# A new start for a fused decoder trunk: c spread by one DMA, x scaled on ScalarE, first scale and shift columns on ScalarE, products of zeros ahead

## The chip, the cores and the metric

The kernel runs on one core of one Trainium2 chip. The metric is device time in microseconds (us) of one execution. One execution is also taken by the hardware profiler; its span and the trace behind it are what the text reads. The engines have short names: PE is the matrix engine (PEld its weight loads), DVE the vector engine, ACT the scalar (activation) engine, POOL the general one, SP the engine whose queue issues most DMAs. Each works through its own instructions in the order in which they were written, and waits where an operand is not ready.

## What is computed

Two layers of a decoder trunk act on x (256 x 1024, fp32). A vector c (1024) gives, through silu and one matrix per layer, nine vectors of 1024: a shift, a scale and a gate for each of three sub-layers. Cut to what matters:

```python
mod = (jax.nn.silu(c) @ mod_w[l] + mod_b[l]).reshape(bsz, N_SUB, 3, D_MODEL)
def pre(x_in, i):                       # before each sub-layer
    return rms_norm(x_in, norm_pre[l, i]) * (1.0 + mod[:, i, 1]) + mod[:, i, 0]
def post_add(x_in, y, i, res_w):        # after it
    return x_in + res_w * mod[:, i, 2] * rms_norm(y, norm_post[l, i])
x = post_add(x, swiglu(pre(x, 0), ffn_w_in[l, 0], ffn_w_out[l, 0]), 0, FFN_RES)
y = token_mixer(pre(x, 1), ...)         # S5 scan and forgetting attention
x = post_add(x, y, 1, 1.0)
x = post_add(x, swiglu(pre(x, 2), ffn_w_in[l, 1], ffn_w_out[l, 1]), 2, FFN_RES)
```

`rms_norm` divides each row by its root mean square; `swiglu` is `(silu(h @ gate) * (h @ up)) @ w_out` with an inner width of 2816.

## The kernel before

**Weights.** Everything that is multiplied comes in one stream of 512 pieces of 128 x 1024 floats (512 KB), issued by SP in the order of `stream_order`. A weight piece (`fi`: into a feed-forward layer, `fo`: out of it, and others) lands in a tile `raw`; ACT copies it to a rounded tile `hi`, DVE takes the rest, `lo = raw - hi`. Each product is three matmuls (`mm3`): hi by hi, hi by lo, lo by hi, on the activations' own pair `xh`, `xl`. A modulation piece (`mod`) is not multiplied on PE: `mod_piece` multiplies it on DVE with silu(c), which stands in all 128 partitions as the tile `crow`, and sums along the row, which gives one column of 128 numbers in the tile `mc`. Column `8+k` of `mc` is block k of the first scale, column `k` of the first shift.

**The first stage.** `run` loads c, x (two tiles of 128 rows), an identity matrix, and the stream. c comes as one row and PE spreads it over the partitions, by a matmul with a row of ones into a PSUM tile `c`, which ACT turns into `crow`. Each half of x is squared and summed (ACT for the first, DVE for the second), POOL makes the reciprocal root, DVE multiplies it in (`xn`), PE transposes `xn` in blocks of 128 columns into two PSUM tiles `xnt`, and ACT copies these to SBUF (`keep`). The first feed-forward layer's input needs 16 modulation pieces, two for each block k; the stream has them between the first 16 `fi` pieces, one after each. When both of a block are done, `first_block(k)` finishes its two columns on DVE (`mod_finish`: bias, 1 + scale, times the norm's weight), and ACT makes `xh` and `xf`, the scaled and shifted block, rounded and not; DVE takes `xl = xf - xh`. `ffn_first` then multiplies: four output tiles f (units 0 to 3), each from four pieces j = 0 to 3, and piece j needs the blocks 2j and 2j+1. For one j all four units are done before the next j. So PE's order is fi of units 0, 1, 2, 3 for j = 0, then for j = 1, and so on, 24 matmuls of 256 columns each. After these 16 pieces come the first `fo` products into y, and the rest of the layer.

**What sets the order.** A planner (`Plan`) writes the instructions out. It keeps an estimated clock for each engine, and when PE's clock moves on it lets the task run whose engine is free and whose inputs are estimated to be ready; tasks are the splits of the stream (`hi`, `lo`, `mod`), `first_block`, and the scalar work of the S5 branch (`s5t` tiles: many small operations on 128 x 32, at a lower priority, placed where DVE is estimated to be idle). On the chip the order is fixed; waits are for the data. `Stream.pump` issues DMAs as long as fewer than `RAW` = 11 pieces are held.

All operations of the planner's engines are recorded at one line of the profile, L127, so that groups are told apart by their tiles' names.

Of the kernel before, what the change touches and what calls it, by code (L numbers as in the profile page):

```python
# [39 lines left out]
TICKS = (1, 2)  # L40
FIRST = 1
TURN = 0.8
SLACK = 0.3
HASTE = 0.9
NEAR = 1
# [240 lines left out]
class Later:  # L286
# [36 lines left out]
class Stream:  # L323
# [31 lines left out]
            return None, 0.0  # L355
        return "act", self.plan.ready([self.raw[0][1]])

    def hi(self):
        key, t = self.raw.pop(0)
        hi = self.kb.r4("hi", F32R)  # L360
        self.kb.nc.scalar.activation(hi, t, AF.Copy)
        self.split.append((key, t, hi))
        self.pump()

# [45 lines left out]
class Kern:  # L410
# [164 lines left out]
    def first_block(self, k):  # L575

        nc = self.nc
        yield "dve",
        for r in range(2):
            self.mod_finish(0, 0, r, slice(k, k + 1))  # L580
        f = self.r4("xf")[:, 0:256].rearrange("p (m t) -> p m t", m=2)
        src = self.xnt[k // 4][:, k % 4]
        a, b = self.mc[:, 8 + k:9 + k], self.mc[:, k:k + 1]
        nc.scalar.activation(self.xh[:, :, k, :], src, AF.Identity, bias=b, scale=a)
        nc.scalar.activation(f, src, AF.Identity, bias=b, scale=a)
        yield "dve", self.plan.clk["act"] + self.plan.LATENCY
        nc.vector.tensor_tensor(self.xl[:, :, k, :], f, self.xh[:, :, k, :], op=ALU.subtract)
        for m in range(2):
            self.x_done(m, k)
# [1127 lines left out]
    def run(self):  # L1717
        tc, nc, I = self.tc, self.nc, self.I
        pool = tc.tile_pool
        with (tc.manual_schedule(engines=ENG), pool(name="cst", bufs=1) as cst, pool(name="r4p", bufs=SLOTS) as self.r4p,  # L1720
# [16 lines left out]
            self.mc = cst.tile([P, 144], F32, name="mc")  # L1737
            self.plan.untimed = {t.tensor.name for t in (self.xh, self.xl, self.mc)}
            self.mhalf = cst.tile([P, 1], F32, name="mhalf")
            wfh = cst.tile([P, 2, 64], F32R, name="wfh")  # L1740
            wfl = cst.tile([P, 2, 64], F32R, name="wfl")
            cst.tile([P, 8], F32, name="pad")
            crow, one = self.r4("c0"), self.r4("one")
            nc.sync.dma_start(crow[0:1, :], I["c"])
            nc.sync.dma_start(self.x[0], I["x"][0])
            nc.sync.dma_start(self.ident, I["cm"][:, 3, :])
            nc.sync.dma_start(self.x[1], I["x"][1])
            self.st = Stream(self, I["ws"], self.order)
            self.st.pump(2)
            nc.sync.dma_start(cols, I["cols"])  # L1750
            nc.sync.dma_start(self.s5p, I["s5p"])
            self.st.pump()
            self.mb, self.npre, self.npost = cols[:, 0:144], cols[:, 144:192], cols[:, 192:240]
# [5 lines left out]
            for l in range(2):  # L1759
# [10 lines left out]
            nc.gpsimd.memset(one[0:1, 0:P], 1.0)  # L1770
            nc.scalar.activation(self.crow[:, 0:1], self.mhalf, AF.Silu)
            ps = self.psum("c")
            for h in range(2):
                nc.tensor.matmul(ps[:, 512 * h:512 * h + 512], one[0:1, 0:P], crow[0:1, 512 * h:512 * h + 512],
                                 start=True, stop=True)
            xn = [self.r4("xn") for m in range(2)]
            ss = [self.sumsq(self.x[0], xn[0], "ssx"), self.sm("ssx")]
            nc.scalar.activation(self.crow, ps, AF.Silu)
            nc.vector.scalar_tensor_tensor(xn[1], self.x[1], 1.0, self.x[1], op0=ALU.mult, op1=ALU.mult,
                                           accum_out=ss[1][:, 0:1])  # L1780
            pt = [self.psum("xnt").rearrange("p (k m t) -> p k m t", k=4, m=2) for _ in range(2)]
            for m in range(2):
                r = self.rstd(ss[m])
                nc.vector.tensor_scalar(xn[m], self.x[m], r, None, op0=ALU.mult)
                for k in range(8):
                    nc.tensor.transpose(pt[k // 4][:, k % 4, m, :], xn[m][:, k * P:k * P + P], self.ident)
            self.xnt = [self.r4("xnt").rearrange("p (k m t) -> p k m t", k=4, m=2) for _ in range(2)]

            def keep(h, src):
                yield "act", src  # L1790
                nc.scalar.activation(self.xnt[h], src, AF.Copy)
# [4 lines left out]
            ss = ps = pt = xn = crow = one = None  # L1796
# [16 lines left out]
            xn = [None, None]  # L1813
            for g in range(6):
# [14 lines left out]
                xn = [self.r4(f"xn{m}") for m in range(2)]  # L1829
# [91 lines left out]
```

## Time and profile before

| | us |
|---|---|
| median of 3 runs (lowest, highest) | 1189.62 (1188.34, 1194.59) |
| the profiled execution | 1197.85 |
| its span, first to last instruction | 1196.1 |
| PE busy in the span | 1153.5 (96%) |
| DVE busy | 906.5 (76%) |
| ACT busy | 605.5 (51%) |
| POOL busy | 34.3 (3%) |
| PE busy in the first of 40 slices (29.9 us each), in the second | 60 to 69%, 90% or more |

The profiled execution is 8.2 us longer than the median; 1.75 us of it lie outside the span. Durations below come from this execution. A row of the timeline reads: start, duration, engine, line, operation, output tile <- input tiles, shapes, how many are merged in the row, and in square brackets the idle time before it with what ended the wait. An instruction's duration includes the time to empty its pipeline, so that the next on the same engine can start before it ends; the pace is read from start to start. A busy PE is modelled, so that short stalls of the products show in the gaps of starts rather than in busy time.

### The profile page before, as it was taken

To read this page: it belongs to the slowest core of one execution; us is meant where nothing else is said; L and a number is where in the kernel's file an instruction comes from. 1 tells how busy PE (TensorE), PEld (TensorE's weight loads), DVE (VectorE), ACT (ScalarE), POOL (GpSimd) and SP (SyncE) were. 2 spreads that over 40 slices of the span, in tenths; PEclk is the share of its full clock that TensorE was granted. 3 is DMA by queue.
4 is the path that set the end of the run, shared out by engine and by line. 5 is a ranking of instruction groups with operands and counts; after the bars stand their busy time and mean duration, and the time that the engine had idled before them with its cause. 6 is when DMAs were issued, how large, how long until landed. Compare 5 with 4: busy or idle time off the path is not lost.

```text
span 1196.1 us, 19360 instructions
## 1 busy us (share of the span) xinstructions
PE 1153.5 (96%) x7476; PEld 1031.8 (86%) x7476; DVE 906.5 (76%) x1518; ACT 605.5 (51%) x920; POOL 34.3 (3%) x61
## 2 busy tenths in 40 slices
PE   6999999998989999999999999999999999999997
PEld 5899998797778879999988989987987887999995
DVE  6899888798696889999768878878447598855532
ACT  4454553585456465444445476356355757543430
POOL 1000000000000010000010000001000001000000
PEclk9999999999797999999999999999999999999998
DMA  9999886567967569999758488967635556765300
GB/s 355 408 367 359 313 299 231 188 242 243 355 239 284 195 222 380 368 369 399 269 206 328 170 289 271 411 206 264 232 122 185 184 203 211 281 220 204 124 19 35
DMA packets 99474, 306.50 MB, mean 256 GB/s; under 512 B 16533, under 2 KB 26421, under 8 KB 99382
## 3 DMA queue, kind: packets, MB, share of 16 engines
q1 hardware_dynamic: 99382, 305.27, 70.2%
q8 instruction: 58, 0.95, 0.3%
q14 instruction: 34, 0.28, 0.1%
HBM read 291.51 MB, written 13.71 MB: 255 GB/s over the span
## 4 chain that ended last, share of the span: by engine, by line
PE 78%; DVE 10%; ACT 5%; DMA 4%; issue 2%; SPq 1%; POOL 1%; DVEq 0%; POOLq 0%; ACTq 0%
PE f L127 32%; PE y L127 18%; PE z L127 4%; PE ym L127 3%; DMA raw<-ws 3%; PE n L127 3%; PE ga L127 2%; DVE lo L127 2%; PE q L127 2%; PE k L127 2%; ACT xh L127 2%; PE ys L127 2%; PE u L127 2%; PE v L127 1%; PE yb L127 1%
## 5 line engine op out<-in xcount | busy, mean ns | idle before, releaser
L127 DVE TENSOR_TENSOR lo<-raw,hi 128x1024 fp32r<-128x1024 f32 x368 | 436.3, 1218 | 36.0 <-ACT hi L127 19.2
L127 ACT ACTIVATE hi<-raw 128x1024 fp32r<-128x1024 f32 x368 | 370.7, 1055 | 73.0 <-PE f L127 39.5
L127 PE MATMUL f<-xh,hi 128*128 128x256 f32 x1216 | 344.0, 283 | 3.1 <-ACT xh L127 3.1
L127 PE MATMUL f<-xl,hi 128*128 128x256 f32 x1216 | 343.4, 282 | 2.5 <-DVE xl L127 2.5
L127 PE MATMUL f<-xh,lo 128*128 128x256 f32 x1216 | 343.0, 282 | 1.1 <-DVE lo L127 1.1
L127 PEld LDWEIGHTS f<-xh,lo 128*128 128x128 f32 x1216 | 234.0, 192 | 1.7 <-DVE lo L127 1.7
L127 PEld LDWEIGHTS f<-xh,hi 128*128 128x128 f32 x1216 | 230.4, 189 | 5.4 <-ACT xh L127 4.2
L127 PEld LDWEIGHTS f<-xl,hi 128*128 128x128 f32 x1216 | 230.1, 189 | 4.7 <-DVE xl L127 3.7
L127 PE MATMUL y<-hi,ht 128*128 128x512 f32 x704 | 197.4, 393 | 0.8 <-DVE yg L127 0.8
L127 DVE SCALAR_TENSOR_TENSOR raw<-raw,crow 128x1024 f32<-128x1024 f32 x144 | 173.4, 1219 | 13.1 <-DMA raw<-ws 13.1
L127 PEld LDWEIGHTS y<-hi,ht 128*128 128x128 f32 x704 | 129.8, 189 | 26.3 <-DVE yg L127 1.1
L127 ACT ACTIVATE sg<-f 128x512 f32<-128x512 f32 x38 | 22.7, 598 | 217.9 <-PE f L127 210.4
L127 PE MATMUL y<-lo,ht 128*128 128x512 f32 x352 | 109.9, 391 | 0.8 <-ACT yg L127 0.8
L127 DVE TENSOR_TENSOR sg<-sg,f 128x512 f32<-128x512 f32 x38 | 26.1, 687 | 84.1 <-ACT sg L127 84.1
L127 PEld LDWEIGHTS y<-lo,ht 128*128 128x128 f32 x352 | 66.3, 189 | 15.4 <-ACT yg L127 1.2
L127 PE MATMUL n<-hi,xl 128*128 128x512 f32 x96 | 37.9, 395 | 1.7 <-DVE xl L127 1.7
L127 ACT ACTIVATE lg<-lg,st 128x128 f32<-128x128 f32 (+1 forms) x64 | 26.1, 444 | 25.2 <-DVE st L127 25.2
L127 PE MATMUL n<-hi,xh 128*128 128x512 f32 x96 | 38.4, 400 | 0.0
L127 PE MATMUL n<-lo,xh 128*128 128x512 f32 x96 | 37.7, 392 | 0.0
L127 DVE TENSOR_TENSOR yg<-y,row 128x1024 f32<-128x1024 f32 (+1 forms) x9 | 9.9, 1103 | 31.9 <-ACT xn L127 20.9
L127 DVE TENSOR_TENSOR ht<-sg,ht 128x512 fp32r<-128x512 f32 x38 | 26.1, 688 | 9.3 <-ACT ht L127 9.0
L127 ACT ACTIVATE xh<-xt,mc 128x128 fp32r<-128x128 f32 x80 | 21.7, 383 | 22.0 <-PE xt L127 22.0
(268 smaller groups left out, 1658.3 us busy)
## 6 DMA issues: line engine op xcount, KB each, us to landing
raw<-ws SPq DMA_DIRECT2D x512, 512.0 KB, 5.9
row<-sg SPq DMA_DIRECT2D x11, 512.0 KB, 6.5
sbt<-bT SPq DMA_DIRECT2D x8, 512.0 KB, 3.1
sc<-cd SPq DMA_DIRECT2D x16, 256.0 KB, 7.8
bt<-sbt SPq DMA_DIRECT2D x8, 512.0 KB, 4.9
c<-sc SPq DMA_DIRECT2D x8, 512.0 KB, 7.1
d<-sd SPq DMA_DIRECT2D x4, 512.0 KB, 7.5
w<-sw SPq DMA_DIRECT2D x4, 512.0 KB, 3.8
```

Source lines behind the costliest of these rows:

```text
L127: r = f(*a, **k)
```

## The change

Seven edits, all but one in the program's start:

1. c is read by one DMA that repeats its row for all 128 partitions, straight into `crow`; ACT takes silu in place. The matmul with ones, its PSUM tile and the row of ones go.
2. x's scaling by the reciprocal root (`xn`) moves from DVE to ACT, for both halves.
3. The DMAs of the identity matrix and of the columns of biases and norm weights (`cols`) move from SP's queue to ACT's.
4. `first_block` no longer finishes its columns on DVE in three small operations; ACT does it in two, with `pre` = (1 + bias) * norm weight, which POOL prepares once. The planner now counts on 1.0 us (`FRESH`) instead of 0.2 us (`LATENCY`) from ACT's end until DVE takes `xl`.
5. The transposed x is read from PSUM by the first block; the copies to SBUF come after it.
6. The first two modulation pieces and the first `fi` piece's split are written out by hand, ahead of the planner, and that one piece is rounded by DVE, not by ACT.
7. PE starts with six products of zeros (`warm`, 128 x 512, in fp32, 12 instructions as the two before were four), which nothing reads.

```diff
+FRESH = 1.0
+WARM = 6
...
-    def hi(self):
+    def hi(self, early=False):
         key, t = self.raw.pop(0)
         hi = self.kb.r4("hi", F32R)
-        self.kb.nc.scalar.activation(hi, t, AF.Copy)
+        if early:
+            self.kb.nc.vector.tensor_copy(hi, t)
+        else:
+            self.kb.nc.scalar.activation(hi, t, AF.Copy)
...
     def first_block(self, k):
-        yield "dve",
-        for r in range(2):
-            self.mod_finish(0, 0, r, slice(k, k + 1))
+        yield "act", self.plan.clk["dve"] + self.plan.LATENCY
...
         a, b = self.mc[:, 8 + k:9 + k], self.mc[:, k:k + 1]
+        nc.scalar.activation(a, a, AF.Identity, bias=self.pre[:, k:k + 1], scale=self.npre[:, k:k + 1])
+        nc.scalar.activation(b, b, AF.Identity, bias=self.mb[:, k:k + 1])
         nc.scalar.activation(self.xh[:, :, k, :], src, AF.Identity, bias=b, scale=a)
         nc.scalar.activation(f, src, AF.Identity, bias=b, scale=a)
-        yield "dve", self.plan.clk["act"] + self.plan.LATENCY
+        yield "dve", self.plan.clk["act"] + FRESH
         nc.vector.tensor_tensor(self.xl[:, :, k, :], f, self.xh[:, :, k, :], op=ALU.subtract)
...
-            nc.sync.dma_start(crow[0:1, :], I["c"])
-            nc.sync.dma_start(self.x[0], I["x"][0])
-            nc.sync.dma_start(self.ident, I["cm"][:, 3, :])
-            nc.sync.dma_start(self.x[1], I["x"][1])
+            nc.sync.dma_start(self.crow, I["c"].to_broadcast([P, D]))
+            for m in range(2):
+                nc.sync.dma_start(self.x[m], I["x"][m])
+            for t, src in ((self.ident, I["cm"][:, 3, :]), (cols, I["cols"])):
+                tc.nc.scalar.dma_start(t, src)
             self.st = Stream(self, I["ws"], self.order)
-            self.st.pump(2)
-            nc.sync.dma_start(cols, I["cols"])
+            self.st.pump(5)
...
-            for h in range(2):
-                nc.tensor.matmul(ps[:, 512 * h:512 * h + 512], one[0:1, 0:P], crow[0:1, 512 * h:512 * h + 512],
-                                 start=True, stop=True)
+            ps = self.psum("warm")
+            for i in range(WARM):
+                nc.tensor.matmul(ps[:, 0:512], warm[:, 0:P], warm[:, 0:512], start=True, stop=True)
             xn = [self.r4("xn") for m in range(2)]
+            nc.scalar.activation(self.crow, self.crow, AF.Silu)
             ss = [self.sumsq(self.x[0], xn[0], "ssx"), self.sm("ssx")]
-            nc.scalar.activation(self.crow, ps, AF.Silu)
...
-                nc.vector.tensor_scalar(xn[m], self.x[m], r, None, op0=ALU.mult)
+                nc.scalar.activation(xn[m], self.x[m], AF.Copy, scale=r)
...
+            nc.gpsimd.tensor_scalar(self.pre, cols[:, 8:16], 1.0, None, op0=ALU.add)
+            nc.gpsimd.tensor_tensor(self.pre, self.pre, cols[:, 144:152], op=ALU.mult)
+            self.st.mod()
+            self.st.mod()
+            self.st.hi(True)
+            self.st.lo()
             self.plan.busy = False
```

The planner's clocks move with these edits, so the order of instructions changes on DVE as far as the first mixer of layer 0, and a little on ACT and SP; PE's order is the same but for its first row. Three places show it. In the rows, `raw` with `mc` is a modulation piece, `lo` the rest of a weight piece, `s5t` the S5 scalars.

DVE at the start of the program, before:

```order
L127 SCALAR_TENSOR_TENSOR xn_157,ssx_160<-x_70 128x1024
L127 TENSOR_SCALAR xn_156<-x_69,ssx_158 128x1024
L127 TENSOR_SCALAR xn_157<-x_70,ssx_160 128x1024
L127 SCALAR_TENSOR_TENSOR raw_3_95,mc<-raw_3_95,crow 128x1024
L127 SCALAR_TENSOR_TENSOR raw_4_97,mc<-raw_4_97,crow 128x1024
L127 TENSOR_TENSOR mc<-mc,cols 128x1 x2
L127 SCALAR_TENSOR_TENSOR mc<-mc,cols 128x1
L127 TENSOR_TENSOR lo_214<-raw_5_101,hi_204 128x1024
L127 TENSOR_TENSOR xl<-xf_211,xh 128x2x128
```

and with the change:

```order
L129 MEMSET warm_89 128x512
L129 SCALAR_TENSOR_TENSOR xn_160,ssx_164<-x_70 128x1024
L129 SCALAR_TENSOR_TENSOR raw_2_95,mc<-raw_2_95,crow 128x1024
L129 SCALAR_TENSOR_TENSOR raw_3_97,mc<-raw_3_97,crow 128x1024
L129 CAST hi_199<-raw_4_99 128x1024
L129 TENSOR_TENSOR lo_203<-raw_4_99,hi_199 128x1024
L129 TENSOR_TENSOR xl<-xf_212,xh 128x2x128
```

The two scalings and the three column operations are gone from it, a rounding and the filling with zeros are new.

DVE in the middle of the first stage, from the `xl` of one block to that of the next, before (blocks 4 and 5):

```order
L127 TENSOR_TENSOR xl<-xf_460,xh 128x2x128
L127 TENSOR_TENSOR lo_476<-raw_41_256,hi_444 128x1024
L127 SCALAR_TENSOR_TENSOR raw_42_263,mc<-raw_42_263,crow 128x1024
L127 TENSOR_TENSOR lo_503<-raw_44_290,hi_484 128x1024
L127 SCALAR_TENSOR_TENSOR raw_46_295,mc<-raw_46_295,crow 128x1024
L127 TENSOR_TENSOR mc<-mc,cols 128x1 x2
L127 SCALAR_TENSOR_TENSOR mc<-mc,cols 128x1
L127 TENSOR_TENSOR xl<-xf_537,xh 128x2x128
```

and with the change (up to blocks 2 and 6):

```order
L129 TENSOR_TENSOR lo_273<-raw_9_110,hi_256 128x1024
L129 SCALAR_TENSOR_TENSOR raw_10_112,mc<-raw_10_112,crow 128x1024
L129 SCALAR_TENSOR_TENSOR s5t_207<-s5t_207 128x32
L129 TENSOR_SCALAR s5t_207<-s5t_207 128x32
L129 SCALAR_TENSOR_TENSOR s5t_207<-s5t_207 128x32 x3
L129 TENSOR_TENSOR lo_323<-raw_11_114,hi_294 128x1024
L129 TENSOR_TENSOR xl<-xf_312,xh 128x2x128
```

```order
L129 TENSOR_TENSOR lo_573<-raw_52_371,hi_567 128x1024
L129 SCALAR_TENSOR_TENSOR raw_54_380,mc<-raw_54_380,crow 128x1024
L129 SCALAR_TENSOR_TENSOR s5t_207<-s5t_207 128x32
L129 TENSOR_SCALAR s5t_207<-s5t_207 128x32 x2
L129 SCALAR_TENSOR_TENSOR s5t_207<-s5t_207 128x32
L129 TENSOR_SCALAR s5t_207<-s5t_207 128x32
L129 TENSOR_TENSOR lo_623<-raw_57_413,hi_595 128x1024
L129 TENSOR_TENSOR xl<-xf_613,xh 128x2x128
```

Between the second modulation piece of a block and its `xl` stood the three column operations; now five S5 operations and the `lo` of the next piece stand there. This holds for the blocks 1, 2, 3 (with the S5 operations ahead of the `lo`), 4, 6 and 7; at block 5 a `lo` and a modulation piece stand there.

ACT at the start, with the change (before: `hi` and the copy of `xnt` stood ahead of the first `xh`, and `crow` behind the squares of x):

```order
L129 ACTIVATE crow<-crow 128x1024
L129 ACTIVATE xn_159,ssx_162<-x_69 128x1024
L129 ACTIVATE xn_159<-x_69,ssx_162 128x1024
L129 ACTIVATE xn_160<-x_70,ssx_164 128x1024
L129 ACTIVATE mc<-mc,pre,cols 128x1
L129 ACTIVATE mc<-mc,cols 128x1
L129 ACTIVATE xh<-xnt_166,mc 128x2x128
L129 ACTIVATE xf_212<-xnt_166,mc 128x256
L129 ACTIVATE xnt_217<-xnt_166 128x1024
L129 ACTIVATE xnt_219<-xnt_167 128x1024
L129 ACTIVATE hi_240<-raw_7_106 128x1024
```

The scalings stand behind the sums of squares, and the column operations behind the scalings; the `hi` of the second piece comes after all of them.

More of the change, by code (lines that the diff above doesn't have):

```diff
@@ L1739, in run @@
             self.mhalf = cst.tile([P, 1], F32, name="mhalf")
+            self.pre = cst.tile([P, 8], F32, name="pre")
             wfh = cst.tile([P, 2, 64], F32R, name="wfh")
             wfl = cst.tile([P, 2, 64], F32R, name="wfl")
-            cst.tile([P, 8], F32, name="pad")
-            crow, one = self.r4("c0"), self.r4("one")
-            nc.sync.dma_start(crow[0:1, :], I["c"])
-            nc.sync.dma_start(self.x[0], I["x"][0])
-            nc.sync.dma_start(self.ident, I["cm"][:, 3, :])
-            nc.sync.dma_start(self.x[1], I["x"][1])
+            warm = self.r4("warm")
+            nc.sync.dma_start(self.crow, I["c"].to_broadcast([P, D]))
[3 more added lines that the diff above has]
+                tc.nc.scalar.dma_start(t, src)
+                self.plan.times[t.tensor.name] = 4.0, "dma"
             self.st = Stream(self, I["ws"], self.order)
-            self.st.pump(2)
-            nc.sync.dma_start(cols, I["cols"])
+            self.st.pump(5)
             nc.sync.dma_start(self.s5p, I["s5p"])
@@ L1769, in run @@
             self.plan.busy = True
-            nc.gpsimd.memset(one[0:1, 0:P], 1.0)
-            nc.scalar.activation(self.crow[:, 0:1], self.mhalf, AF.Silu)
-            ps = self.psum("c")
-            for h in range(2):
-                nc.tensor.matmul(ps[:, 512 * h:512 * h + 512], one[0:1, 0:P], crow[0:1, 512 * h:512 * h + 512],
-                                 start=True, stop=True)
+            nc.vector.memset(warm[:, 0:512], 0.0)
+            nc.scalar.activation(self.mc[:, 0:1], self.mhalf, AF.Silu)
+            ps = self.psum("warm")
+            for i in range(WARM):
+                nc.tensor.matmul(ps[:, 0:512], warm[:, 0:P], warm[:, 0:512], start=True, stop=True)
             xn = [self.r4("xn") for m in range(2)]
+            nc.scalar.activation(self.crow, self.crow, AF.Silu)
             ss = [self.sumsq(self.x[0], xn[0], "ssx"), self.sm("ssx")]
-            nc.scalar.activation(self.crow, ps, AF.Silu)
             nc.vector.scalar_tensor_tensor(xn[1], self.x[1], 1.0, self.x[1], op0=ALU.mult, op1=ALU.mult,
@@ L1783, in run @@
                 r = self.rstd(ss[m])
-                nc.vector.tensor_scalar(xn[m], self.x[m], r, None, op0=ALU.mult)
+                nc.scalar.activation(xn[m], self.x[m], AF.Copy, scale=r)
                 for k in range(8):
                     nc.tensor.transpose(pt[k // 4][:, k % 4, m, :], xn[m][:, k * P:k * P + P], self.ident)
-            self.xnt = [self.r4("xnt").rearrange("p (k m t) -> p k m t", k=4, m=2) for _ in range(2)]
+            self.xnt = list(pt)
             def keep(h, src):
                 yield "act", src
-                nc.scalar.activation(self.xnt[h], src, AF.Copy)
+                t = self.r4("xnt").rearrange("p (k m t) -> p k m t", k=4, m=2)
+                nc.scalar.activation(t, src, AF.Copy)
+                self.xnt[h] = t
             for h in range(2):
@@ L1795, in run @@
             nc.gpsimd.tensor_scalar(cols[:, 144:240], cols[:, 144:240], ROOT, None, op0=ALU.mult)
-            ss = ps = pt = xn = crow = one = None
+            nc.gpsimd.tensor_scalar(self.pre, cols[:, 8:16], 1.0, None, op0=ALU.add)
+            nc.gpsimd.tensor_tensor(self.pre, self.pre, cols[:, 144:152], op=ALU.mult)
+            ss = ps = pt = xn = warm = None
+            self.st.mod()
+            self.st.mod()
+            self.st.hi(True)
+            self.st.lo()
             self.plan.busy = False
```

## The prediction

> **What bounds the kernel now.** First the busy time by stage (columns: stretch, its length, busy time and count of PE, PEld, DVE, ACT, POOL, clock, DMA share, GB/s):
>
> ```profile
> 0.00:15.10 15.10, 7.42 (x20) 4.43 (x20) 5.83 (x12) 6.09 (x9) 3.21 (x11) 1.00 0.85 305
> 15.10:71.20 56.10, 51.05 (x387) 48.67 (x388) 47.38 (x89) 28.92 (x41) 0.18 (x1) 1.00 1.02 395
> 71.20:120.00 48.80, 48.80 (x352) 45.76 (x351) 45.21 (x98) 21.77 (x26) 0.00 (x0) 1.00 0.97 366
> 120.00:205.00 85.00, 85.00 (x566) 78.31 (x566) 74.69 (x168) 39.21 (x46) 1.30 (x2) 1.00 0.77 275
> 205.00:400.00 195.00, 182.19 (x1086) 156.68 (x1085) 159.31 (x322) 116.10 (x217) 4.33 (x8) 0.90 0.72 255
> ```
>
> From 71.2 to 205 us PE has no gap at all: it is the bound, and what is won before reaches at least to 205. Before 71.2 it is not. Then the timeline around the last block of the first stage, DVE, ACT and PE:
>
> ```profile
> 54.00 0.42 DVE L127 TENSOR_TENSOR xl<-xf,xh 128x256 fp32r<-128x256 f32 x1 [1.16 <-ACT xf L127]
> 54.35 1.22 DVE L127 TENSOR_TENSOR lo<-raw,hi 128x1024 fp32r<-128x1024 f32 x1
> 55.48 1.22 DVE L127 SCALAR_TENSOR_TENSOR raw<-raw,crow 128x1024 f32<-128x1024 f32 x1
> 56.63 1.22 DVE L127 TENSOR_TENSOR lo<-raw,hi 128x1024 fp32r<-128x1024 f32 x1
> 57.77 1.22 DVE L127 SCALAR_TENSOR_TENSOR raw<-raw,crow 128x1024 f32<-128x1024 f32 x1
> 59.02 0.23 DVE L127 TENSOR_TENSOR mc<-mc,cols 128x1 f32<-128x1 f32 x2
> 59.29 0.16 DVE L127 SCALAR_TENSOR_TENSOR mc<-mc,cols 128x1 f32<-128x1 f32 x1
> 59.49 0.60 ACT L127 ACTIVATE xh<-xnt,mc 128x256 fp32r<-128x256 f32 x1 [3.62 <-DVE mc L127]
> 59.99 0.59 ACT L127 ACTIVATE xf<-xnt,mc 128x256 f32<-128x256 f32 x1
> 60.61 0.42 DVE L127 TENSOR_TENSOR xl<-xf,xh 128x256 fp32r<-128x256 f32 x1 [1.16 <-ACT xf L127]
> 61.09 0.39 PE L127 MATMUL f<-xl,hi 128*128 128x256 f32 x1 [0.56 <-DVE xl L127]
> 61.31 0.28 PE L127 MATMUL f<-xh,lo 128*128 128x256 f32 x1
> 70.50 0.28 PE L127 MATMUL f<-xh,lo 128*128 128x256 f32 x1
> 70.62 0.62 PE L127 MATMUL y<-hi,ht 128*128 128x512 f32 x2
> ```
>
> DVE sets the pace: from `xl` to `xl` 6.61 us, which are 0.35 to the next start, four large operations at 1.14, 0.54 (58.91 to 59.45) for the accumulator and the three column operations, 1.16 of idle until ACT's `xf` is there. PE needs for the two pieces of such a period 48 matmuls at 0.113 us (61.31 to 70.50 is 81 steps in 9.19 us), 5.4 us, and waits for `xl`. After the last `xl` it has 9.5 us left, without a gap, to 70.62.
>
> **The change, part by part.** *The pace.* Seven periods lie between the first `xl` and the last (the first row is below, at 15.81), 44.8 us before: 26 large operations 29.6, seven times 0.54 and 1.16 are 11.9, 7 x 0.35 is 2.5, and five S5 operations, from these rows 0.84:
>
> ```profile
> 29.36 0.26 DVE L127 TENSOR_SCALAR s5t<-s5p 128x32 f32<-128x32 f32 x2
> 29.66 0.40 DVE L127 TENSOR_SCALAR s5t<-s5t 128x32 f32<-128x32 f32 x2
> 30.09 0.19 DVE L127 SCALAR_TENSOR_TENSOR s5t<-s5t 128x32 f32<-128x32 f32 x1
> 30.20 1.23 DVE L127 TENSOR_TENSOR lo<-raw,hi 128x1024 fp32r<-128x1024 f32 x1
> ```
>
> In the new order I count 13 `lo`, 14 modulation pieces and 35 S5 operations: 27 x 1.14 + 35 x 0.168 + 2.5 = 39.1 us. The column work is then on ACT: two operations on one column. The nearest row is 0.20 us,
>
> ```profile
> 2.01 0.20 ACT L127 ACTIVATE crow<-mhalf 128x1 f32<-128x1 f32 x1
> ```
>
> so `xf` ends about 0.05 + 0.40 + 0.05 + 0.50 + 0.59 = 1.6 us after the modulation piece. DVE has 0.84 + 1.14 = 2.0 us of other work there (2.3 at block 5): the wait is covered. Without that cover it would be 1.6 us a block instead of 1.16. Saving in the pace: 5.7 us. If each small ACT operation took 0.4, 0.0 to 0.1 a block would show, 0.7 in all. Behind ACT's new wait for DVE stand the two `hi` of the next period; their `lo` follow `xl` by at least one modulation piece, 1.14 + 0.35 us, against 1.05 for a `hi`: hidden.
>
> *The start.*
>
> ```profile
> 2.47 3.75 PE L127 MATMUL c<-c,one 1*128 1x512 f32 x4 [2.47 <-DMA c<-c]
> 4.77 1.06 ACT L127 ACTIVATE xn<-x 128x1024 f32<-128x1024 f32 x1 [2.56 <-DMA x<-x]
> 7.85 1.23 DVE L127 SCALAR_TENSOR_TENSOR xn<-x 128x1024 f32<-128x1024 f32 x1 [7.85 <-DMA x<-x]
> 10.52 0.76 DVE L127 TENSOR_SCALAR xn<-x,ssx 128x1024 f32<-128x1024 f32 x1 [0.77 <-POOL ssx L127]
> 9.81 3.67 PE L127 MATMUL xnt<-ident,xn 128*128 128x128 f32 x16 [3.59 <-DVE xn L127]
> 15.81 0.42 DVE L127 TENSOR_TENSOR xl<-xf,xh 128x256 fp32r<-128x256 f32 x1
> ```
>
> x's halves landed at 4.77 and 7.85. Ahead of them now stand 512 KB of c instead of 4 KB. A piece takes 0.524 MB at the 410 GB/s of the steady stream, 1.28 us:
>
> ```profile
> DMA packets 2245, 8.19 MB, mean 410 GB/s; under 512 B 248, under 2 KB 248, under 8 KB 2244
> ```
>
> So the second lands at 7.85 + 1.28 = 9.1 if the queue's start-up stays as it is, and at about 7.9 if c only fills the hole at the start (305 GB/s over the first 15.1 us above, not 410). I take 9.1. ACT's chain: 9.1, 2.67 until the root is there (7.85 to 10.52), 1.0 for the scaling, where DVE took 0.76, four transposes at 0.21 (16 of them take 3.67 with a pause between the halves) with 0.2 to PSUM, `xh` at 13.9, `xf` done at 15.0. DVE's chain: 1.15 for the squares, two modulation pieces 2.4, the rounding 0.76 (the scalings' duration; as slow as a `lo` at most, 1.14), `lo` 1.14, together 14.6 to 15.0. So the first `xl` starts at 15.0 instead of 15.81: 0.8 won, with 0 to 2.0 as bounds. DVE's two scalings and ACT's copy leave the path, but c's 1.28 us and ACT's slower scaling take most of it back. POOL's column work comes after the second root (11.8) and has until 13.5, where ACT takes it up: three operations on up to 96 columns, which I leave at nothing; 0.5 late would be the worst. The identity and `cols`, on ACT's queue, are issued before c can land, and there nothing waits behind them. c, first in the queue, should land 0.4 ahead of x's first half now, near 4.4; its silu takes as long as a scaling, 1.0, and its reader comes at 10.3: hidden by 4.8 us.
>
> *PE.* The last `xl` starts at 15.0 + 39.1 = 54.1, 6.5 us earlier. PE then is nearly the bound itself, and its first products run at half rate, as now:
>
> ```profile
> 24.62 0.41 PE L127 MATMUL f<-xl,hi 128*128 128x256 f32 x1
> 24.83 0.41 PE L127 MATMUL f<-xh,lo 128*128 128x256 f32 x1
> 26.12 0.28 PE L127 MATMUL f<-xh,hi 128*128 128x256 f32 x1
> 26.23 0.28 PE L127 MATMUL f<-xl,hi 128*128 128x256 f32 x1
> ```
>
> Steps of 0.21 us become 0.11 near 25.8; the window rows say a clock of 1.00 throughout, but the recorded clock begins only there, so the steps decide. I assume the same moment. By then 12 matmuls of block 0 have run, a wait until the second `xl` (19.7), 12 of block 1, and 17 of the next piece. The other 343 of 384 take 38.8 us: 64.6. Warm from the start, PE would still wait for blocks 2, 4 and 5, and end at 64.5. So the zeros are worth next to nothing here, and f ends at 64.6 instead of 70.6: **6.0 us won**, 5.5 for a late x, 7.2 for an early one.
>
> Would the zeros keep the clock? The windows around another gap speak against it (columns: stretch, length, PE busy and count, clock, DMA share, GB/s):
>
> ```profile
> 210.17:213.59 3.42, 1.51 (x9) 1.00 0.81 331
> 213.59:217.00 3.41, 3.41 (x9) 0.50 0.02 8
> ```
>
> A stretch of 3.4 us in which PE was 44% busy was followed by one at 0.50. After the zeros PE has 3.4 us of transposes at most until 14, in 5 us, so I count on half rate. The Trainium skill, "TensorE: Matmul & The Clock Gate", "What's actually happening", has the clock fall only after an idle window of some 3.4 us; by that it would stay up, and the sum would be 64.5 instead of 64.6. The rows above differ from it: half a window of work was not enough.
>
> *Behind the stage.* DMAs no longer lead by as much: 1.3 us later, their readers 6 earlier. The first `fo` is the 34th piece of the stream. DVE took the first piece at 11.19,
>
> ```profile
> 11.19 1.28 DVE L127 SCALAR_TENSOR_TENSOR raw<-raw,crow 128x1024 f32<-128x1024 f32 x1
> 66.10 1.05 ACT L127 ACTIVATE hi<-raw 128x1024 fp32r<-128x1024 f32 x1
> ```
>
> so by 11.19 + 33 x 1.28 = 53.4 the first `fo` was there, and ACT touched it at 66.10: over 12 us of slack, 5 left. DVE has more room than before: it ends the stage 6.5 us earlier with 30 S5 operations and one `lo` more behind it. So nothing takes the 6.0 us before 205. In the mixer (205 to 400), PE is idle 12.8 us and DVE busy for 82%; S5 operations done early can give up to 1.5 us, a changed order on DVE take as much. I add 0.5. Saving 6.5 us: the profiled execution goes from 1197.85 to 1191.4, the median of the runs, 8.2 below, from 1189.62 to 1183.1.
>
> **The rivals.**
> *A late start, about 3.5 us won, 1186.1.* x lands at 11 instead of 9.1, because ACT's queue shares the engines and each new DMA has slow first packets, or the six products of zeros, 12 instructions at the 0.94 us at which the four of c run, hold PE until 12.5 and the transposes with it. For it: those four take 3.75 us, and PE is at the slow clock then; against it: PE speeds up within 11 us of work here. Then the first `xl` comes at 17 to 17.5 and f ends near 67.
> *More than counted, 8.5 us, 1181.1.* c fills the hole of the start, x lands at 7.9, f ends at 63.3 (7.2 won), and the S5 tables come earlier by 1.3 us. For it: 305 GB/s at the start; against it: the hole lies where first packets of x are slow.
> *Given back later, 0 to 2 us, 1188.6.* The stage ends early, but the mixer's DVE chain, in new order, puts S5 operations ahead of the norm chain on which PE waits. For it: DVE is 82% busy there; against it: these operations are about 0.4 us each.
> *Slower, 1196.9.* 128 reads of one row of 4 KB go one after another. At 0.16 us for each (0.524 MB in 1.28 us on 16 engines is 0.16 for a packet of 4 KB), 20.5 in all, c would land near 22.5 instead of 4.4; it decides from 15.2 on (4.4, plus 4.8 of cover, plus the 6.0 won). The loss would be 22.5 - 15.2 = 7.3. Against it: a repeated row from memory, issued alone late in the kernel at 1141.63, flows at up to 455 GB/s:
>
> ```profile
> GB/s 0 0 0 0 0 0 0 0 146 273 455 328 419 309 146 146 91 18 0 0 0 0 73 0 0 0 0 0 0 0 0 0 0 0 0 0 0 0 0 0
> ```
>
> (40 slices of 0.225 us from 1141.0), over within 3.5 us.
>
> **How the numbers follow.** The forecast has 0.47, a late start 0.22, more than counted 0.16, given back 0.10, slower 0.05. What a measurement can tell here is 0.5%, 5.9 us; the limits are 1183.7 and 1195.6. The forecast, at 6.5 with a width of 1.5, lies beyond it by a little more than half (0.29), the second rival nearly always (0.15), and some of the first and third by luck of the runs (0.06): faster 0.50. Slower keeps 0.05, the same 0.45. The range 1178.5 to 1190.0 holds the first two cases and the third nearly whole, most of the fourth, and none of the last.
>
> **What would show it.** Right: the last of the eight `xl` near 54 us, no idle time of over 0.3 us ahead of the later ones, a first `xl` at 15, the first y product at 64 to 65, no PE gap from there to 199. Wrong: an idle time ahead of the `xl` (ACT's columns cost more), a wait for DMA ahead of the modulation pieces (the stream became the bound), a first `xl` later than 15.8, or an unchanged first y product.

## The result, and the profile after

The change takes 1185.24 us (median of 20 runs, 1182.43 to 1191.41), the kernel before 1189.70 beside it (20 runs, 1186.92 to 1202.51): a ratio of 0.9949, with an interval of 0.9927 to 0.9970. The gain is 4.5 us (by the interval 3.6 to 8.7); 6.5 were forecast (1183.1). The profiled execution after has a span of 1185.3 us, before 1196.1. That difference of 10.8 is not the gain: by the recorded clock before's execution spent 34 us of the mixer at half rate (292 to 374), the change's 24 (288 to 363), and before's time of 1197.85 lies far above its median. So the stages are compared by their marks below, and the time by the medians.

The start after the change, from the timeline (columns: start, duration, engine, line, operation, idle time before and what ended it):

```profile
1.44 7.16 PE L129 MATMUL warm<-warm 128*128 128x512 f32 x12 [1.44 <-DVE warm L129]
8.84 1.23 DVE L129 SCALAR_TENSOR_TENSOR xn<-x 128x1024 f32<-128x1024 f32 x1 [7.46 <-DMA x<-x]
9.03 1.46 POOL L129 TENSOR_TENSOR ssx<-ssx,mhalf 128x1 f32<-128x1 f32 x1
10.19 1.23 DVE L129 SCALAR_TENSOR_TENSOR raw<-raw,crow 128x1024 f32<-128x1024 f32 x1
10.47 1.01 POOL L129 TENSOR_SCALAR ssx<-ssx 128x1 f32<-128x1 f32 x1
11.40 1.23 DVE L129 SCALAR_TENSOR_TENSOR raw<-raw,crow 128x1024 f32<-128x1024 f32 x1
11.57 1.84 POOL L129 TENSOR_TENSOR ssx<-ssx,mhalf 128x1 f32<-128x1 f32 x1
12.68 0.69 DVE L129 CAST hi<-raw 128x1024 fp32r<-128x1024 f32 x1
13.44 1.15 ACT L129 ACTIVATE xn<-x,ssx 128x1024 f32<-128x1024 f32 x1 [1.77 <-POOL ssx L129]
14.65 1.97 PE L129 MATMUL xnt<-ident,xn 128*128 128x128 f32 x8 [0.98 <-ACT xn L129]
15.06 0.39 ACT L129 ACTIVATE mc<-mc,pre,cols 128x1 f32<-128x1 f32 x1 [0.47 <-DMA s5p<-s5p]
15.35 0.28 ACT L129 ACTIVATE mc<-mc,cols 128x1 f32<-128x1 f32 x1
16.91 0.43 DVE L129 TENSOR_TENSOR xl<-xf,xh 128x256 fp32r<-128x256 f32 x1 [2.28 <-ACT xf L129]
```

x's second half is there at 8.8, but its root, two operations on a single column, is ready only at 13.41. The power takes 1.84 us, the sum ahead of it 1.01. Each of GpSimd's three rows ends shortly after a VectorE operation beside it: 10.49 after 10.07 (the squares of x), 11.48 after 11.42 (the first modulation piece), 13.41 after 13.37 (the rounding `hi`). The first `xl` comes at 16.91, not at 15.0 (before: 15.81).

The rest of the stage, from the same timeline:

```profile
45.76 0.42 DVE L129 TENSOR_TENSOR xl<-xf,xh 128x256 fp32r<-128x256 f32 x1
46.24 0.39 PE L129 MATMUL f<-xl,hi 128*128 128x256 f32 x1 [0.59 <-DVE xl L129]
55.55 0.41 DVE L129 TENSOR_TENSOR xl<-xf,xh 128x256 fp32r<-128x256 f32 x1
66.64 0.39 PE L129 MATMUL y<-hi,ht 128*128 128x512 f32 x1
```

No later `xl` waits; seven periods take 55.55 - 16.91 = 38.64 us (before 44.80). PE waits for the last time at block 5, and then runs without a pause to the first y product at 66.64 (before 70.62). Behind it (columns: stretch, length, busy time and count of PE, PEld, DVE, ACT, POOL, clock, DMA share, GB/s):

```profile
65.00:71.20 6.20, 6.20 (x37) 5.41 (x37) 5.82 (x8) 6.20 (x9) 0.00 (x0) 1.00 0.99 326
71.20:120.00 48.80, 48.80 (x355) 46.27 (x354) 42.16 (x103) 19.57 (x24) 0.00 (x0) 1.00 1.02 393
120.00:205.00 85.00, 85.00 (x562) 78.17 (x561) 73.55 (x137) 37.64 (x45) 1.59 (x4) 1.00 0.80 287
```

PE has no gap there, so the 3.98 us won by the first y product reach the mixer whole.

### The profile page after: what moved, and what is told of

Read it like the earlier page. It is cut to its first block, busy times and chain, and to the rows that moved or that the text cites. A ratio compares the mean times of both kernels' runs of the same rounds, so it can differ in the third digit from the quotient of the medians.

```text
span 1185.3 us, 19360 instructions
## 1 busy us (share of the span) xinstructions
PE 1148.1 (97%) x7484; PEld 1025.8 (87%) x7484; DVE 903.6 (76%) x1494; ACT 610.8 (52%) x937; POOL 36.8 (3%) x62
## 4 chain that ended last, share of the span: by engine, by line
PE 82%; DVE 9%; ACT 4%; DMA 2%; issue 1%; POOL 1%; DVEq 0%; POOLq 0%; ACTq 0%; SPq 0%
PE f L129 35%; PE y L129 20%; PE n L129 5%; PE z L129 4%; PE ym L129 3%; PE ga L129 3%; PE v L129 2%; PE q L129 2%; PE k L129 2%; PE ys L129 2%; PE u L129 2%; DVE lo L129 2%; ACT xh L129 1%; DVE zi L129 1%; DVE raw L129 1%
## 5 line engine op out<-in xcount | busy, mean ns | idle before, releaser
L129 ACT ACTIVATE sg<-f 128x512 f32<-128x512 f32 x38 | 22.7, 597 | 225.5 <-PE f L129 218.1
L129 ACT ACTIVATE lg<-lg,st 128x128 f32<-128x128 f32 (+1 forms) x64 | 26.1, 443 | 25.4 <-DVE st L129 25.4
L129 DVE SCALAR_TENSOR_TENSOR xl<-xt,mc,xh 128x128 fp32r<-128x128 f32 x80 | 21.7, 344 | 15.7 <-ACT xh L129 15.7
```

The costliest lines, as they stand in the source:

```text
L129: r = f(*a, **k)
```

## The experiments

All times of marks are microseconds from the start of the span. The table collects them from the timelines of all runs; the first y product is the end of the first stage's inner products.

| run | first xl | third xl | last xl | first y | time (runs) |
|---|---|---|---|---|---|
| before | 15.81 | 26.74 | 60.61 | 70.62 | 1189.70 (20) |
| the change | 16.91 | 27.41 | 55.55 | 66.64 | 1185.24 (20) |
| no zeros | 16.70 | 27.19 | 55.31 | 66.66 | 1188.62 (1) |
| pace alone | 15.29 | 25.83 | 54.47 | 65.59 | 1209.77 (1) |
| pace alone, three transfers on GpSimd's queue | 15.83 | 26.37 | 55.02 | 65.00 | 1204.33 (1) |
| start alone | 18.44 | 29.37 | 63.23 | 73.23 | 1193.73 (1) |
| silu(c) in PSUM | 14.66 | 25.16 | 53.28 | 65.16 | 1180.74 (1) |
| the same again | 14.33 | 25.02 | 53.15 | 64.23 | 1182.82 (12) |
| + x loaded first | 17.12 | 27.81 | 56.44 | 66.44 | 1182.66 (1) |
| + x and squares first | 15.36 | 25.86 | 53.99 | 65.86 | 1183.55 (1) |
| + more zeros | 14.48 | 27.17 | 55.32 | 66.46 | 1181.67 (1) |
| + more zeros, order kept | 14.37 | 25.00 | 53.15 | 65.02 | 1183.22 (9) |
| + S5 work behind the stage | 14.42 | 25.00 | 51.82 | 64.14 | 1210.18 (1) |
| the change again | 16.78 | 27.27 | 55.40 | 66.50 | 1185.95 (12) |

Single times of one kernel differ by several us, so the marks decide, not they.

### Who holds the root: silu(c) in PSUM

The theory: GpSimd is held while VectorE runs an operation with two inputs in SBUF. The edit takes one of the two inputs of the first two modulation pieces out of SBUF and, but for one more silu on ACT, changes nothing in the order:

```
+pc = self.psum("pc")
+nc.scalar.activation(pc, self.crow, AF.Silu)
 ss = [self.sumsq(self.x[0], xn[0], "ssx"), self.sm("ssx")]
...
 nc.scalar.activation(self.crow, self.crow, AF.Silu)      # later, for the pieces behind
...
+(self.crow is pc while these two are written)
 self.st.mod()
 self.st.mod()
```

> The change, with the one edit that the first two modulation pieces read silu(c) from PSUM and not from SBUF (ACT writes it there as well, in a gap of its own); their order and all else is the same. Theory A (GpSimd is locked out while VectorE runs an operation with two inputs in SBUF): the second root, which took 10.47 to 13.41 us beside the two pieces, becomes as fast as beside an operation that reads PSUM: 0.22 for the sum and 0.57 for the power after the first root ends near 10.5, so ACT's second scaling starts at 11.3 to 11.7 and not at 13.44; the first xl starts at 14.7 to 15.2 (DVE's own chain ends at 14.6), the first y product comes near 64.9 and not at 66.64. Theory B (GpSimd's first powers of a program are slow by themselves, whatever VectorE does): second scaling at 13.4, first xl at 16.9, first y at 66.6. Theory C (x arrives too late or ACT's scaling and its column operations set the start): the root is early, the first xl moves by less than 0.5 us.

The same place in its timeline:

```profile
8.46 1.22 DVE L129 SCALAR_TENSOR_TENSOR xn<-x 128x1024 f32<-128x1024 f32 x1 [7.08 <-DMA x<-x]
8.68 1.43 POOL L129 TENSOR_TENSOR ssx<-ssx,mhalf 128x1 f32<-128x1 f32 x1
9.86 1.22 DVE L129 SCALAR_TENSOR_TENSOR raw<-raw,pc 128x1024 f32<-128x1024 f32 x1 [0.17 <-DMA raw<-ws]
10.09 0.21 POOL L129 TENSOR_SCALAR ssx<-ssx 128x1 f32<-128x1 f32 x1
10.39 0.56 POOL L129 TENSOR_TENSOR ssx<-ssx,mhalf 128x1 f32<-128x1 f32 x1
14.66 0.43 DVE L129 TENSOR_TENSOR xl<-xf,xh 128x256 fp32r<-128x256 f32 x1 [0.36 <-ACT xf L129]
```

VectorE's modulation piece takes 1.22 us in both kernels and runs beside the root in both; only where its second input lies is new. The sum falls from 1.01 to 0.21 us, the power from 1.84 to 0.56. The first root still runs beside the squares of x, which read x twice from SBUF, and still takes 1.43. That is theory A and rules out slow first powers. The Trainium skill, "SBUF — State Buffer", section "SBUF: two separate sides", describes just this: the port pair that VectorE and GpSimd share is an exclusive lock, taken by a VectorE operation with two SBUF inputs against a GpSimd operation that reads SBUF; the rows agree. From the squares of x to the second root it is now 2.5 us (8.46 to 10.95) and not 4.6 (8.84 to 13.41). The first `xl` comes 2.25 us earlier (14.66), about as expected; x had landed 0.4 earlier here as well. The first y product came at 65.16, 0.3 later than expected, of which more at the end.

Two inputs are not the only case in these traces: before the change, the sum ran beside VectorE's scaling of x (9.00 to 9.75), which has one input, and took 0.66 us; the power behind it had VectorE idle beside it.

```profile
9.17 0.66 POOL L127 TENSOR_SCALAR ssx<-ssx 128x1 f32<-128x1 f32 x1 [2.29 <-DVE xn L127]
9.91 0.57 POOL L127 TENSOR_TENSOR ssx<-ssx,mhalf 128x1 f32<-128x1 f32 x1
```

The change's power, too, ended only behind the rounding, which has one input. How much of the 1.84 us is the rounding's share no run separates.

### The zeros

```
-WARM = 6
+WARM = 0
```

> The change without its products of zeros. Prediction's step (zeros worth next to nothing): the matmul steps of the first blocks are 0.21 us until about 25.5 as with zeros, the first xl stays at 16.9, the first y at 66.6 (within 0.3). Rival A (the zeros hold PE and delay the transposes): the transposes start earlier than 11.73. Rival B (the zeros bring the clock up earlier): without them the rate of 0.11 comes later than 25.5, and the first y by over 0.5 us later.

The transposes started at 11.52 instead of 11.73, as everything ahead of them came 0.2 earlier, the first `xl` at 16.70, the first y product at 66.66. Full rate came later without them, as rival B had it (the steps of 0.21 us last until 27.5, with the zeros until 25.4), but the first y product did not. In the change the six products neither hold PE nor help: they end at 8.6, PE is nearly idle in the next window, and the clock falls at 11.80, before the first f product (columns as above, of the change):

```profile
8.38:11.80 3.42, 0.29 (x2) 0.08 (x2) 2.85 (x5) 1.40 (x3) 2.92 (x4) 1.00 1.03 417
11.80:25.45 13.65, 11.04 (x45) 9.49 (x46) 11.19 (x22) 9.39 (x16) 3.14 (x4) 0.50 1.03 409
```

The fall at 11.80 is not seen in every execution. The recorded clock changes at the edges of stretches of some 3.4 us, which lie elsewhere each time: in the second execution of the run with silu(c) in PSUM, which has the same six products, it stayed full until 20.6. So one run without zeros can't tell whether the later full rate is their doing.

### The two halves of the change, each alone

The pace alone is the kernel before with `first_block` as changed, and `pre` made on GpSimd. The start alone is the change with `first_block` as before:

```
-yield "act", self.plan.clk["dve"] + self.plan.LATENCY
+yield "dve",
+for r in range(2):
+    self.mod_finish(0, 0, r, slice(k, k + 1))
...
-nc.scalar.activation(a, a, AF.Identity, bias=self.pre[:, k:k + 1], scale=self.npre[:, k:k + 1])
-nc.scalar.activation(b, b, AF.Identity, bias=self.mb[:, k:k + 1])
...
-yield "dve", self.plan.clk["act"] + FRESH
+yield "dve", self.plan.clk["act"] + self.plan.LATENCY
```

> The kernel before with the column work on ACT alone (accumulator columns scaled by two ACT operations, the product of columns that it needs on GpSimd, the due time of xl at 1.0 as in the change); loads and start as before. Theory A (the whole gain is the pace; the new start costs 1.1 us): first xl at 15.8, seven periods in 38.5 to 39.5, last xl at 54.3 to 55.3, first y at 65.0 to 65.8, so about 1.2 us earlier than in the change. Theory B (the pace needs the new start's loads and its early rounding): periods over 41, first y after 67.

> The change with its start (loads, scaling on ACT, zeros, rounding of the first piece on VectorE), but with the column work of the blocks on VectorE as before. Theory A: first xl at 16.5 to 17.2, seven periods near 44.8 as before, last xl near 61.7, first y at 71.0 to 72.0: later than before (70.62), the start by itself loses. Prediction's step: first xl near 15.0, first y near 69.8.

The pace alone brings the first y product to 65.59, 5.03 us earlier than before and 1.05 earlier than the change. Seven periods take 39.18. So the pace carries the whole gain of the stage. The start alone loses even more than expected, 2.61 us (73.23): besides the root, ACT there copies both `xnt` tiles ahead of the first block.

```profile
15.49 1.94 ACT L129 ACTIVATE xnt<-xnt 128x1024 f32<-128x1024 f32 x2 [1.20 <-PE xnt L129]
17.32 0.60 ACT L129 ACTIVATE xh<-xnt,mc 128x256 fp32r<-128x256 f32 x1
18.44 0.43 DVE L129 TENSOR_TENSOR xl<-xf,xh 128x256 fp32r<-128x256 f32 x1 [3.70 <-ACT xf L129]
```

With the column work on VectorE the planner makes ACT's part of the first block due later, and the copies go first; in the change they follow it. That part is an effect of the order, not of the loads; how the 2.61 us divide between the root and the copies was not measured.

### Where the pace alone loses 20 us later

It takes 1209.77 us all the same. It was still 0.96 us ahead of the change at 278 us. Its first `sc<-ident,lg` product came at 309.0, 14.8 later than in the change, and the span ended 22.7 later (1208.0 against 1185.3). Its chain of waits there (start, duration, work):

```profile
285.39 8.62 DMA snb<-cumt
...
295.82 7.97 DMA raw<-ws
303.81 1.24 DVE lo L128
305.09 4.11 PE gb L128 x11
```

and SP's queue:

```profile
285.39 0.44 SPq L128 DMA_DIRECT2D snb<-cumt  x1
294.03 0.33 SPq L128 DMA_DIRECT2D nbp<-snb  x1
294.93 3.21 SPq L128 DMA_DIRECT2D raw<-ws  x6
```

VectorE had written `cumt` at 273.2, but in this plan its store stands behind 22 other transfers on SP. Its reader `nbp` then holds SP until 294, and the weights are issued after that. In the change the same store is issued at 270.60, its reader at 275.21 and the weights behind it from 278.34 on. The next run keeps the order and issues these three transfers from GpSimd's queue, in both layers (`q = Timed(self.plan, "dma", self.tc.nc.gpsimd)` in `forget_rows`).

> The kernel with the pace edit alone, which won 5.0 us in the first stage and was 20 us behind the change by 330 us; its order on the engines is kept, but the three transfers of the forget gate's row (snb<-cumt, nbp<-snb, nbd<-snb) are issued from GpSimd's queue and not from SP's. Theory A (the loss sits in SP's queue: in this plan the store snb<-cumt stands behind 22 transfers of kt, bt and d and is issued 12.3 us after cumt is written, its two readers block SP until 294, and five weight loads stand behind them): the store is issued within 2 us of cumt, the weight loads behind go out near 286 instead of 294.9, the gap of PE of some 8 us around 300 goes, and the end comes at 1185 to 1198 in place of 1208. Theory B (the clock or VectorE's order causes the loss): the end stays within 3 us of 1208.

```profile
272.85 0.76 POOL L128 DMA_DIRECT2D snb<-cumt  x1 [57.95 <-DVE pw L128]
286.81 5.20 SPq L128 DMA_DIRECT2D raw<-ws  x6
```

and in its windows:

```profile
310.00:320.00 10.00, 10.00 (x49) 10.00 (x48) 9.44 (x17) 2.19 (x8) 1.16 (x2) 0.50 1.02 410
```

The store goes out at once, the weights 8.1 us earlier, and the mark at 309.0 moves to 301.4. So 7.6 of the 14.8 us there are SP's queue. The other 7.2 are not lost time for the most part: in this plan PE's own order differs from the change's between 235 and 371 us, and 48 products of `ga` and `gb`, which the change runs later, stand ahead of that mark. Counted by the number of products done, the pace alone is 8.4 us behind the change there, and the run with the other queue 0.8.

The end moves only from 1208.0 to 1202.6, outside both expectations. PE stands still for 3.93 us until 309.22, ahead of its first `vi` product (for what, the profile does not show), and its clock is at half rate from 308 to 325, where the change ran at full rate. Where the other 17 us at the end lie one by one, stays open; PE's other order is a cause that no run tested.

### Is x late, or VectorE's own chain?

Two runs load x's halves ahead of c, both with silu(c) in PSUM; the second also puts ACT's squares ahead of silu.

```
-nc.sync.dma_start(self.crow, I["c"].to_broadcast([P, D]))
 for m in range(2):
     nc.sync.dma_start(self.x[m], I["x"][m])
+nc.sync.dma_start(self.crow, I["c"].to_broadcast([P, D]))
...                        second run:
+ss = [self.sumsq(self.x[0], xn[0], "ssx"), self.sm("ssx")]
 nc.scalar.activation(pc, self.crow, AF.Silu)
 nc.scalar.activation(self.crow, self.crow, AF.Silu)
-ss = [self.sumsq(self.x[0], xn[0], "ssx"), self.sm("ssx")]
```

> The run with silu(c) in PSUM, and x's two halves loaded ahead of c. Theory A (with the lock gone VectorE's own chain sets the first xl: modulation pieces as they land, the rounding, lo): x's second half lands near 7.3 and not at 8.46, both roots are done by 9.8, the first xl stays within 0.3 of 14.66, because the first two pieces of the stream still land near 9.8 and 11.1. Theory B (x's arrival sets the start, as the prediction's sum over ACT's chain had it): first xl near 13.4, 1.2 us earlier.

> The run with silu(c) in PSUM, with x's halves loaded ahead of c and ACT's squares ahead of silu as well (in the run with the loads alone moved, ACT's squares waited behind silu for c until 9.24). Theory A (VectorE's chain behind the stream's first pieces sets the first xl): x's second half is there near 6.2, the second root by 9.3, two scalings on ACT until 12.5, the first xl at 13.9 to 14.7, so at most 0.7 earlier than 14.66. Theory B (x's arrival sets the start): first xl at 13.4 or earlier.

Both expectations of both runs missed. In the first, the squares stood behind the silu on ACT, and this now waited for c:

```profile
8.28 1.03 ACT L129 ACTIVATE pc<-crow 128x1024 f32<-128x1024 f32 x1 [5.14 <-DMA crow<-c]
9.24 1.04 ACT L129 ACTIVATE xn<-x 128x1024 f32<-128x1024 f32 x1
13.06 1.28 POOL L129 TENSOR_SCALAR pre<-cols 128x8 f32<-128x8 f32 x1
15.46 0.39 ACT L129 ACTIVATE mc<-mc,pre,cols 128x1 f32<-128x1 f32 x1 [1.89 <-POOL pre L129]
```

The late first root put GpSimd's column work beside VectorE's `lo` and third modulation piece, both with two inputs in SBUF. The two operations on `pre` took 1.28 and 1.01 us, not 0.25 and 0.20 as in the run with silu(c) in PSUM and c first, and ACT waited 1.89 for them. So the delay found at the root came back in the next place.

In the second both roots were done by 8.4, 2.6 us earlier than with c first, yet the first `xl` came 0.7 later:

```profile
7.82 0.56 POOL L129 TENSOR_TENSOR ssx<-ssx,mhalf 128x1 f32<-128x1 f32 x1
10.42 2.17 ACT L129 ACTIVATE xn<-x,ssx 128x1024 f32<-128x1024 f32 x2
11.61 3.46 PE L129 MATMUL xnt<-ident,xn 128*128 128x128 f32 x16 [2.97 <-ACT xn L129]
15.36 0.42 DVE L129 TENSOR_TENSOR xl<-xf,xh 128x256 fp32r<-128x256 f32 x1 [1.08 <-ACT xf L129]
```

The scalings stand behind two silu on ACT (8.40 to 10.42), and the sixteen transposes take 3.46 us at half rate. In the run with silu(c) in PSUM that was timed, at full rate, they took 2.15, and its first `xl` waited for nothing. So x's arrival doesn't set the start: c first was the better order here, and with the root out of the way it is ACT's queue and the transposes at half rate.

### Would more zeros pay?

Nine products at the start in place of six, so that they last until the transposes, and two more where PE waits between the first two blocks; in the second run the planner isn't told of the five added ones.

```
-WARM = 6
+WARM = 9
...
+for n in range(2):      # in ffn_in, behind the first block's products
+    self.nc.tensor.matmul(pss[1][:, 0:512], w[:, 0:P], w[:, 0:512], start=True, stop=True)
```

> The run with silu(c) in PSUM, nine products of zeros at the start in place of six, so that they last until the transposes, and two more between the first block's products and the second's, where PE waits. Theory A (PE has become the bound of the first stage, and its half-rate stretch from 12.3 to 22.6 costs 1 to 1.5 us): the clock stays at full rate, steps of the first block are 0.11 to 0.12, the first xl stays near 14.7, the first y comes at 63.6 to 64.3 instead of 65.16. Theory B (half-filled stretches drop the clock all the same): half rate from about 15 or 19 on, and the first y at 65.2 to 66.5, since zeros at half rate take 3.4 us.

> As the run before with zeros (nine products at the start, two between the first two blocks), but the planner isn't told of the five added products, so VectorE's, ACT's and SP's orders are those of the run with silu(c) in PSUM. There the clock stayed full from 6.6 to 33.9 us, but VectorE had got another order and its third xl came at 27.2 instead of 25.2. Theory A (order took the gain): the xl stand at 14.5, 19.1, 25.0 and 53.1 as without the added zeros (14.66 to 53.28, within 0.3), and the first y comes at 63.2 to 64.3 instead of 65.16, since PE's half-rate stretch until 22.6 is gone. Theory B (zeros are worth nothing even so, because a later wait of PE for xl, half a window long, drops the clock again): one stretch of 3.4 us at 0.50 between 27 and 45, and the first y at 64.6 to 65.4. In time no more than 1.5 us against the run without them.

The clock does hold: full from 6.6 to 33.9 in the first run, from 6.5 to 207.9 in the second. In the first run it fell for one window after PE had been busy for half of the one before:

```profile
30.49:33.90 3.41, 1.69 (x13) 1.29 (x11) 3.27 (x10) 2.62 (x5) 0.00 (x0) 1.00 1.02 407
33.90:37.32 3.42, 3.42 (x19) 3.42 (x18) 3.32 (x9) 1.16 (x2) 0.00 (x0) 0.50 1.03 412
```

The Trainium skill, "TensorE: Matmul & The Clock Gate", section "What's actually happening", has the clock fall after an idle window of some 3.4 us. The window 8.38 to 11.80 of the change was nearly one (0.29 us busy); this one was half full, and the clock fell too, so here an idle window was not needed.

The first run's first y product came late (66.46) since VectorE got another order, and the third `xl` came at 27.17 instead of 25.16. With the order kept the `xl` stand where theory A had them, there is no half-rate stretch, and still the first y product comes at 65.02, not by 64.3. Theory B's time, then, but not for its reason. Two things are behind it. PE, faster at first, waits for VectorE's `xl` (3.0 us in all, up to the one at 43.4). And from 44.1 on its products come every 0.118 us instead of 0.113, at a granted clock of 1.00; over the 180 that are left this is 0.8 us. Full clock from the start is worth nothing measurable here: 1183.22 against 1182.82 us.

### Is PE the bound now?

`s5_scalars` is queued behind the stage (the line moves from `run` to `ffn_first`, behind `self.ffn_in([0, 1, 2, 3])`).

> The run with silu(c) in PSUM, and the scalar S5 operations (35 in the first stage) not queued until the first stage has been written. Theory A (PE is the bound from 22.6 on, at 0.118 a matmul): the xl come at a pace of 33 to 36 us over seven periods instead of 38.6, yet the first y moves by under 0.8 us, 64.4 to 65.2. Theory B (VectorE still sets the pace, 9.5 us from the last xl to the end): the last xl near 48 to 50, the first y near 60 to 62. Behind the stage the S5 operations come later; by how much that costs in the mixer no theory says.

The last `xl` came 1.5 us earlier than with silu(c) in PSUM, the first y product 1.0 earlier (64.14), a little below theory A's 64.4 to 65.2 and far from B. But against the timed run of the same kernel (64.23) it is 0.1. From the second `xl` on, PE waits no more (its last idle ends at 20.35), so PE bounds the stage here. Theory A's pace was missed: the seven periods took 37.4 us, not 33 to 36, though VectorE had 35 operations fewer. It waited instead, 3.1 us ahead of `lo` for ACT's `hi`, and ACT 10.9 us, eight times, for the stream to land the pieces; four of the periods are 5.1 to 5.2 us, where VectorE's own work is 4.9 (four large operations at 1.14, and 0.35) and four pieces at 1.28 take 5.1. The stream moved 407 GB/s over these periods, as much as in its steady stretches. So it comes next: with a start at 14.4, PE, VectorE and the stream lie close together, and work taken from VectorE alone wins next to nothing.

The mixer pays for it: the S5 table `bt` is on its way until 331.6, PE's first `vi` product comes at 331.8, 38 us later than with silu(c) in PSUM, and the span ends 29.5 us later (1208.4 against 1178.9). So the S5 operations that the change puts into the gaps of the first stage are not mere filling: behind the stage they come too late.

### The better kernel, timed

> The change with the first two modulation pieces reading silu(c) from PSUM, timed: from its one run (1180.74 against 1190.44) and the 2.3 us of its first xl, 0.7 to 1.0% below the kernel before, 1179 to 1182 us.

> The change as it is, beside the others on the same chip: 1183 to 1187 us, 0.3 to 0.7% below the kernel before, and 2 to 5 us above the run with silu(c) in PSUM (1.5 us at the first y, 1.5 to 5 by 360 us).

Silu(c) in PSUM: 1182.82 us, a ratio to before of 0.9937 (0.9914 to 0.9959). The change beside it: 1185.95, 0.9958 (0.9937 to 0.9979). The first is just above the 1179 to 1182 us expected, which rested on one run (1180.74); the second is as expected. The 3.1 us between them fit the marks (2.3 at the first y product), but the intervals overlap, so that it beats the change is shown by the marks and not settled by the time.

## Why the prediction was right in time and wrong in one step

**What bounds it, and the pace: right.** VectorE set the pace; the periods fell to 38.64 us, against 39.1 in the sum (the S5 operations took 5.5 us instead of 5.9): 6.2 won instead of 5.7. The wait for ACT's `xf` is gone from every later block. The column operations took 0.39 and 0.28 us, not 0.20 as in the nearest row. The cover of 2.0 us held them all the same, helped by something that the sum did not have: from the third block on only the shorter one stands behind the block's last modulation piece, as the other is done behind the first. (The Trainium skill, "ScalarE: Activation LUTs", section "What ACT_TABLE_LOAD costs", gives 186 ns plus about 93 ns for each operand that is a column; by that they would be an estimated 0.37 and 0.28. These rows agree.)

**The start: wrong, by 1.9 us.** The step that failed is "2.67 until the root is there", taken from 7.85 to 10.52 before. There GpSimd's sum ran beside a scaling with one input, and its power beside no work of VectorE. The change put two modulation pieces, each with two inputs in SBUF, beside that root, and it took 4.60 us (8.84 to 13.44); the run with silu(c) in PSUM shows the cause. The other terms of that chain held: x's second half landed at 8.8 (9.1 forecast), the scaling took 1.15 (1.0), and 14.66 or 14.33 without the lock stands for the 15.0 of the sum. So the new start lost 1.1 us instead of winning 0.8, outside the bounds of 0 to 2.0 won. The prediction's own sign of being wrong, a first `xl` later than 15.8, came true; the time fell into the range all the same, since the pace won its share and the range was wide.

**GpSimd's column work** was put at nothing, 0.5 late at worst. It was held as well (its first operation on `pre` took 1.07 us, 0.25 with silu(c) in PSUM, and the second ended at 15.02), and ACT waited 0.47 for it, but the transposes ended later still: nothing, by luck of the longer delay.

**PE and the zeros: right.** Half rate until 25.45 (25.8 forecast), the zeros worth nothing. The 1.9 us of the late start carry over to the end one to one: 64.6 forecast, 66.64 measured, and 64.23 with the first `xl` at 14.33.

**Behind the stage: right here.** 3.98 us at the first y product and 4.5 in the medians fit, but an interval of 3.6 to 8.7 can't tell whether the 0.5 that was added is real. That nothing is given back holds for this order only, as the pace alone shows: it lost some 7 us where its plan put one small store behind 22 others, and more for causes that stay open.

**The rivals.** The time, 1185.24, lies nearer to the late start (1186.1) than to the forecast, and so do its marks: a first `xl` near 17, the first y product near 67. Its mechanism is not what happened: x was early and the zeros held nothing. Serial reads of c are out, c was there near 5.8. Once the lock is gone the kernel comes out at the forecast itself, 64.23 and 1182.82 against 64.6 and 1183.1, and not at "more than counted" (63.3 and 1181.1).

## What to carry to other kernels

A small operation on GpSimd can take as long as what VectorE does beside it (1.01 us instead of 0.21 here): before moving work of VectorE next to a GpSimd chain, look where its inputs lie. Here one of them in PSUM was enough to free GpSimd. An edit that changes due times in a planned kernel has to be read to its end, since a stage won early can be lost to a queue 200 us later. And where two engines and the stream bound a stage about equally, speeding up one of them shows next to nothing.

## What was not expected of the hardware

The same products come at two steps under the same granted clock of 1.00. In the two executions of one program, silu(c) in PSUM, the first (84 steps) and the second (93 steps) read:

```profile
24.04 0.28 PE L129 MATMUL f<-xh,lo 128*128 128x256 f32 x1
...
33.93 0.28 PE L129 MATMUL f<-xh,lo 128*128 128x256 f32 x1
```

```profile
24.41 0.28 PE L129 MATMUL f<-xl,hi 128*128 128x256 f32 x1
...
34.95 0.28 PE L129 MATMUL f<-xl,hi 128*128 128x256 f32 x1
```

That is 0.118 us and 0.113 us a step. The slower step began at 22.7 in the first, at 33.3 with the pace alone, at 44.1 with the zeros and the order kept. The second kept the faster one through the stage, and so did the change; behind the first y products, from 69.7 and 72.1 on, their f products come at the slower step too, as up to 205 us 90% or more of such products do in every run. Over the stage it is worth up to 1.5 us, as much as some edits tried here, and it explains the 0.9 us between the two executions' first y products: at the 41st f product the first was still 0.1 ahead (24.28 against 24.41). What sets it in is open.
